# Hybrid diffusion trunk on one core: block rows exchanged and PSUM banks joined in the FFN's Strassen pairs, modulation weights and one head's scaling moved to ScalarE in the mixers

## The chip, the cores and the metric

The kernel runs on one core of a Trainium2 chip: TensorE (PE), VectorE (DVE), ScalarE (ACT), GpSimd (POOL) and SyncE (SP, which only issues transfers here), each with its own in-order instruction stream. The metric is the device time of one execution in microseconds (us). The kernel before took 2695.59, 2698.13 and 2703.82 us in three runs, median 2698.13.

## The reference

One inference step of a two-layer trunk with 640 tokens (512 latent, 128 context) of 1024 features. Each layer is a SwiGLU half-step FFN, a token mixer and another half-step FFN. Each of them reads a modulated input and is followed by a weighted residual and a layer norm:

```
def _modulation(cond, w, b):
    return (jax.nn.silu(cond) @ w + b).reshape(cond.shape[0], N_MOD, D_MODEL)

def _ffn_half(x, mod, slot, w1, w3, w2, g, b):
    h = _modulate(x, mod[:, 3 * slot], mod[:, 3 * slot + 1])
    f = (jax.nn.silu(h @ w1) * (h @ w3)) @ w2
    return _residual_post_norm(x, f, mod[:, 3 * slot + 2], FFN_RES, g, b)
```

`w1` and `w3` are 1024 x 2816. The modulation is a 1024 x 9216 product per layer for two conditioning vectors; its weights are streamed beside the other work. The mixer projects the input once, runs three groups of attention heads (A differential, B windowed with a sink logit, C latent) and one output projection. Softmax rows of group B are normalised before they multiply the values.

## The kernel before

**Layout.** Activations lie transposed, features on partitions, so that all 640 tokens are the moving side of every product. An fp32 operand is split into a high and a low part, and each product is three matmuls (`hh,wh`, `hl,wh`, `hh,wl`). The high part of a weight (`wh`) is a cast on ACT and its low part (`wl`, line 306) a subtraction on DVE, in the mixers on POOL.

**An FFN** works through its 22 tiles of 128 hidden features in six chunks, tiles 0-3, 4-6, 7-9, 10-13, 14-17 and 18-21. The first three tiles are plain products. The other 19 are done by class `Pair` (line 830): `w1` and `w3` of a tile are the two rows of a 2 x 2 block matrix, the two halves of the input features are its columns, and the activations are cut into two halves of the features and two of the tokens (`LO`, `HI`, 320 tokens each, `HN`). Seven block products p1 to p7 take the place of eight (Winograd's form), each 12 matmuls of 128x320. TensorE runs them in the order p1, p2, p4, p6, p7, p5, p3. Additions on DVE (line 858) make the four output blocks from the seven products: two of them belong to `w1` and go through SiLU on ACT, and two belong to `w3` and multiply these. The product is split into `gh` (ACT) and `gl` (DVE). After the pairs of a chunk, eight rows of `w2` products (line 485) read `gh` and `gl`; the first two rows are begun before those of the last pair are needed.

**What sets the order of these additions** is a list of deferred steps: `prod` runs `slot()` behind its 12 matmuls, and `slot()` runs each deferred step once, one product late; a step may return the next. `mods(i)` stands three times in a pair and runs the slices of a background task: in the first three of the four FFNs (`nvec`) modulations on DVE, where each `scr` (line 460) multiplies a weight tile by the conditioning and sums it, 0.716 of them a call.

**PSUM.** `bank()` takes one of four single banks in turn, `dbl()` one of two double banks. Before, a pair takes one double bank for p4 and p5, and single banks for p1, p2, p6, p7 and p3.

**A mixer** interleaves attention units with a background of projections. Modulation products (`mod_mm`, line 391) stand between them: each loads the weights of a later unit first (`mod_load`, two transfers of 256 KB, line 374) from the queue in `mod_queue`, which is SP's. SP's stream is in order and also carries weight loads (line 243) and moves between partitions (line 1256), each of which waits for its producer. In a unit of group B, `cb` (line 1715) adds the sink to the row sums, takes the reciprocal and scales the two heads' probabilities `eb` on POOL (line 1719), after which TensorE transposes them (`tr`, line 1133). Step `ptc` (line 1654) copies transposed probabilities of group C out of PSUM on ACT.

Of the kernel before, what the change touches and what calls it, by code (L numbers as in the profile page):

```python
# [105 lines left out]
def trunk_kernel(tc, I, O):  # L106
# [3 lines left out]
    with ExitStack() as es:  # L110
# [30 lines left out]
        def uid():  # L141
            cnt[0] += 1
            return cnt[0]
# [686 lines left out]
        class Pair:  # L830


            def __init__(self, h, tb, last):
# [5 lines left out]
                self.m, self.sl = u(pe_, f"pm{uid()}"), None  # L839
# [5 lines left out]
            def mms(self, out, w, b, k):  # L845
                for i, (a, c) in enumerate(((0, 0), (0, 1), (1, 0))):
                    PE.matmul(out[:, :HN], w[a][:, k, :], b[k][c], start=k == 0 and i == 0, stop=k == 3 and i == 2)  # L847

            def prod(self, out, b, post=None, w=None):
                w = w or ws.get()  # L850
                for k in range(4):
                    self.mms(out, w, b, k)
                slot()
                if post:
                    later.append(post)
# [4 lines left out]
            def c11(self, p2):  # L860
                self.sl = u(pe_, f"sl{uid()}")
                self.op(self.sl[:, LO], self.m[:, LO], p2, ALU.add)
                return lambda: S.activation(self.sl[:, LO], self.sl[:, LO], AF.Silu) and None

            def gate1(self):
                self.op(self.g[:, LO], self.g[:, LO], self.sl, ALU.mult)
                return self.half if self.last else None

            def half(self):
                split(self.gh[:, LO], self.gl[:, LO], self.g[:, LO])  # L870

            def c12(self, p3):
                self.op(self.sl[:, HI], self.m[:, LO], p3, ALU.add)
                return self.silu2

            def silu2(self):
                S.activation(self.sl[:, HI], self.sl[:, HI], AF.Silu)
                return self.gate2

            def gate2(self):  # L880
                V.tensor_tensor(out=self.g[:, HI], in0=self.g[:, HI], in1=self.sl[:, HI], op=ALU.mult)
                return self.hi

            def hi(self):
                c = HI if self.last else slice(0, T)
                S.copy(self.gh[:, c], self.g[:, c])  # L886
                return self.lo

            def lo(self):
                c = HI if self.last else slice(0, T)  # L890
                V.tensor_tensor(out=self.gl[:, c], in0=self.g[:, c], in1=self.gh[:, c].bitcast(F32), op=ALU.subtract)  # L891

            def start(self):
                p1, p2 = bank("p1"), bank("p2")
                self.prod(p1, self.b11, lambda: S.copy(self.m[:, LO], p1[:, :HN]) and None)
                self.prod(p2, self.b21, lambda: self.c11(p2))

            def run(self, mods, begun=False):
                m, op = self.m, self.op
                if not begun:  # L900
                    self.start()
                mods(0)
                p45 = dbl("p4")
                p4, p5 = p45[:, 0, :], p45[:, 1, :]
                self.prod(p4, self.t4)
                p6 = bank("p6")
                self.prod(p6, self.t2, lambda: op(m[:, LO], m[:, LO], p6, ALU.add))
                mods(1)
                p7 = bank("p7")

                def u3():
                    op(m[:, HI], m[:, LO], p7, ALU.add)
                    self.g = u(pe_, f"gf{uid()}")
                    op(self.g[:, LO], m[:, HI], p4, ALU.subtract)
                    return self.gate1
                self.prod(p7, self.t3, u3)

                def u4():
                    op(self.g[:, HI], m[:, HI], p5, ALU.add)
                    op(m[:, LO], m[:, LO], p5, ALU.add)  # L920
                self.prod(p5, self.t1, u4)
                mods(2)
                p3 = bank("p3")
                self.prod(p3, self.b22, lambda: self.c12(p3))

            def run_first(self, mods, other, ts):

                m, op = self.m, self.op
                self.start()
                mods(0)  # L930
                other.start()
                p3 = bank("p3")
                self.prod(p3, self.b22, None, ws.get(4))
                w22 = ws.get(0)
                p45, p6, p7 = dbl("p4"), bank("p6"), bank("p7")
                p4, p5 = p45[:, 0, :], p45[:, 1, :]
                wq = [ws.get(0), ws.get(0), ws.get(2), w22]
                for k in range(4):
                    for o, w, b in zip((p5, p7, p6, p4), wq, (self.t1, self.t3, self.t2, self.t4)):
                        self.mms(o, w, b, k)  # L940
                    mods(k)
                    next(ts, 0)
                slot()

                def post():
                    self.g = u(pe_, f"gf{uid()}")
# [1253 lines left out]
```

## Time and profile before

| | |
|---|---|
| three runs | 2695.59, 2698.13, 2703.82 us |
| the profiled execution | 2705.26 us |
| its span, first to last instruction | 2703.3 us |
| TensorE busy | 2555.0 us, 95% |
| VectorE busy | 2072.3 us, 77% |
| GpSimd busy | 1244.0 us, 46% |
| ScalarE busy | 1175.9 us, 43% |
| mean granted TensorE clock | 0.976 |

A granted clock of 1.00 is 2.4 GHz and 0.50 is 1.2 GHz; a mean between is a mixture of stretches at the two. "Idle before" is the time an engine waited before an instruction, with the instruction or transfer whose end released it. The profiled execution takes 7.1 us more than the median of the three runs.

### The profile page before, as it was taken

The page shows a single profiled execution, that of the slowest core. Times are in us where ns is not written, and L with a number is a line of the kernel's source. Part 1 is how long each engine was busy: PE and PEld are TensorE (multiplying, and loading weights), DVE is VectorE, ACT ScalarE, POOL GpSimd, SP SyncE. Part 2 cuts the span into 40 slices and gives each one's busy share as a digit, 9 for nine tenths or more (in the row PEclk, how much of TensorE's full clock was granted, in tenths as well). Part 3 has the DMA queues.
Part 4 walks back from the last instruction along what each step waited for, and adds up shares of the span by engine and source line. Part 5 has one row for each costly group of instructions (what it writes and reads, how often), then busy time and mean ns, then how long its engine had stood idle before and what let it go on. Part 6 is the DMA issues. An engine that isn't in the chain of part 4 may idle for free. (4 is left out here: it accounts for less than half of the span.)

```text
span 2703.3 us, 49877 instructions
## 1 busy us (share of the span) xinstructions
PE 2555.0 (95%) x18662; PEld 2453.0 (91%) x18662; DVE 2072.3 (77%) x3759; ACT 1175.9 (43%) x2596; POOL 1244.0 (46%) x973
## 2 busy tenths in 40 slices
PE   7999999899999999999989999998998999999997
PEld 6999999888778999999989999998887798999997
DVE  6599889856764879988987998898476558777776
ACT  5233333545575533333353333334545745334333
POOL 2345445522444554544555454454233456435545
PEclk9999999999999999999989999998999999999998
DMA  7333332354344223333222333323543331222222
GB/s 273 116 98 101 111 97 83 117 152 136 91 130 156 71 96 100 103 101 109 68 83 84 112 103 101 110 87 108 158 134 98 103 114 40 82 82 87 79 86 71
DMA packets 130545, 285.89 MB, mean 106 GB/s; under 512 B 16832, under 2 KB 34560, under 8 KB 129664
## 3 DMA queue, kind: packets, MB, share of 16 engines
q1 hardware_dynamic: 130304, 282.70, 33.2%
q8 instruction: 148, 2.42, 0.4%
q14 instruction: 93, 0.76, 0.1%
HBM read 254.95 MB, written 8.81 MB: 98 GB/s over the span
## 5 line engine op out<-in xcount | busy, mean ns | idle before, releaser
L306 DVE TENSOR_TENSOR wl<-wr,wh 128x512 fp32r<-128x512 f32 (+1 forms) x524 | 518.3, 1003 | 74.1 <-ACT wh L299 72.5
L299 ACT CAST wh<-wr 128x512 fp32r<-128x512 f32 (+1 forms) x570 | 333.3, 607 | 479.4 <-DMA wr<-in_w 296.9
L485 PE MATMUL o<-gh,wh 128*128 128x256 f32 (+1 forms) x1408 | 439.5, 312 | 19.4 <-ACT gh L886 11.7
L485 PE MATMUL o<-gl,wh 128*128 128x256 f32 (+1 forms) x1408 | 439.0, 312 | 1.8 <-DVE gl L478 0.3
L485 PE MATMUL o<-gh,wl 128*128 128x256 f32 (+1 forms) x1408 | 436.7, 310 | 0.0
L847 PE MATMUL p<-hh,wh 128*128 128x320 f32 x1216 | 378.4, 311 | 16.8 <-DVE pm L858 16.8
L847 PE MATMUL p<-hl,wh 128*128 128x320 f32 x1216 | 378.2, 311 | 6.2 <-DVE hl L1010 6.2
L847 PE MATMUL p<-hh,wl 128*128 128x320 f32 x1216 | 378.1, 311 | 0.0
L259 POOL TENSOR_TENSOR ws<-wr 128x512 f32<-128x512 f32 x76 | 111.5, 1468 | 545.8 <-DMA wr<-in_w 482.8
L299 ACT CAST wh<-ws 128x512 fp32r<-128x512 f32 x304 | 185.9, 621 | 361.6 <-PE p L847 153.4
L306 POOL TENSOR_TENSOR wl<-ws,wh 128x512 fp32r<-128x512 f32 x152 | 241.3, 1591 | 193.6 <-ACT wh L299 193.1
L610 DVE SCALAR_TENSOR_TENSOR x<-o,gat,x 128x128 f32<-128x128 f32 (+2 forms) x404 | 192.9, 524 | 139.6 <-PE o L485 136.6
L485 PEld LDWEIGHTS o<-gh,wh 128*128 128x128 f32 x1408 | 267.8, 190 | 23.0 <-ACT gh L886 14.5
L485 PEld LDWEIGHTS o<-gl,wh 128*128 128x128 f32 x1408 | 268.1, 190 | 6.7 <-DVE gl L891 4.8
L485 PEld LDWEIGHTS o<-gh,wl 128*128 128x128 f32 x1408 | 267.9, 190 | 0.0
L847 PEld LDWEIGHTS p<-hh,wh 128*128 128x128 f32 x1216 | 229.9, 189 | 19.0 <-issue 18.9
L847 PEld LDWEIGHTS p<-hl,wh 128*128 128x128 f32 x1216 | 230.0, 189 | 7.4 <-DVE hl L1010 7.4
L847 PEld LDWEIGHTS p<-hh,wl 128*128 128x128 f32 x1216 | 230.0, 189 | 0.3 <-DVE wl L306 0.3
L460 DVE SCALAR_TENSOR_TENSOR scr<-wv,cb 128x512 f32<-128x512 f32 x192 | 181.2, 944 | 0.0
L259 POOL TENSOR_TENSOR ws<-wr,wr 128x512 f32<-128x512 f32 x76 | 130.2, 1713 | 0.0
L259 POOL TENSOR_TENSOR ws<-wr,ws 128x512 f32<-128x512 f32 x76 | 129.9, 1709 | 0.0
L259 POOL TENSOR_TENSOR ws<-ws,wr 128x512 f32<-128x512 f32 x76 | 119.1, 1567 | 6.0
(434 smaller groups left out, 6633.9 us busy)
## 6 DMA issues: line engine op xcount, KB each, us to landing
wr<-in_w SPq DMA_DIRECT2D x176, 512.0 KB, 4.2
wm<-in_wmod SPq DMA_DIRECT2D x192, 256.0 KB, 3.9
wr<-in_w SPq DMA_DIRECT2D x128, 256.0 KB, 2.7
wv<-in_wmt SPq DMA_DIRECT2D x96, 256.0 KB, 4.0
wr<-in_w SPq DMA_DIRECT2D x64, 192.0 KB, 2.4
wr<-in_wint SPq DMA_DIRECT2D x24, 512.0 KB, 4.2
wr<-in_wo SPq DMA_DIRECT2D x16, 512.0 KB, 3.8
xd<-x SPq DMA_DIRECT2D x16, 320.0 KB, 5.1
```

The source lines that it names most:

```text
L259: G.tensor_tensor(out=o, in0=x0, in1=x1, op=op)
L299: S.copy(hl[0], src[:, c0:c1])
L306: eng.tensor_tensor(out=t2, in0=src, in1=t.bitcast(F32), op=ALU.subtract)
L460: V.scalar_tensor_tensor(out=scr, in0=w[2 * i + hf], scalar=1.0, in1=cb[:, 2 * st + hf, :], op0=ALU.mult, op1=ALU.mult, accum_out=a[:, 2 * ...
L485: PE.matmul(out[:, :cn], whl[a][:, k, :], b[:, c0:c0 + cn], start=k == 0 and i == 0, stop=k == n - 1 and i == 2)
L610: V.scalar_tensor_tensor(out=c, in0=src, scalar=gat[:, d, s:s + 1], in1=c, op0=ALU.mult, op1=ALU.add)
L847: PE.matmul(out[:, :HN], w[a][:, k, :], b[k][c], start=k == 0 and i == 0, stop=k == 3 and i == 2)
```

## The change

Five edits. (1) A pair is loaded with its two block rows exchanged (`tw[::-1]`), so that the first finished output block (from p1 and p2) and the last (from p3) belong to `w3`, and the two between to `w1`, which alone go through SiLU. The step behind p3 is now an addition and the multiplication in one. (2) p6 and p7 share a double bank as p4 and p5 do, and a pair takes both double banks, p6's first. (3) In the last pair of a chunk the second and third call of `mods` hold the `scr` steps; their credit is kept and is spent in the rows that follow. (4) In the mixers the modulation weights are loaded from ACT's queue, and two units' loads are issued ahead of the background. (5) `cb` scales the first head on ACT and the second on POOL. Functions that nothing calls any more go.

```
-                self.m, self.sl = u(pe_, f"pm{uid()}"), None
+                self.m = u(pe_, f"pm{uid()}")
...
-                self.prod(p1, self.b11, lambda: S.copy(self.m[:, LO], p1[:, :HN]) and None)
-                self.prod(p2, self.b21, lambda: self.c11(p2))
...
+                def c11():
+                    self.g = u(pe_, f"gf{uid()}")
+                    op(self.g[:, LO], m[:, LO], p2, ALU.add)
+                self.prod(p1, self.b11, lambda: S.copy(m[:, LO], p1[:, :HN]) and None)
+                self.prod(p2, self.b21, c11)
                 mods(0)
-                p45 = dbl("p4")
-                p4, p5 = p45[:, 0, :], p45[:, 1, :]
+                p67, p45 = dbl("p6"), dbl("p4")
+                p4, p5, p6, p7 = (p[:, i, :] for p in (p45, p67) for i in range(2))
                 self.prod(p4, self.t4)
-                p6 = bank("p6")
                 self.prod(p6, self.t2, lambda: op(m[:, LO], m[:, LO], p6, ALU.add))
-                mods(1)
-                p7 = bank("p7")
-
-                def u3():
+                mods(1, self.last)
+
+                def c21():
+                    self.sl = u(pe_, f"sl{uid()}")
                     op(m[:, HI], m[:, LO], p7, ALU.add)
-                    self.g = u(pe_, f"gf{uid()}")
-                    op(self.g[:, LO], m[:, HI], p4, ALU.subtract)
-                    return self.gate1
-                self.prod(p7, self.t3, u3)
-
-                def u4():
-                    op(self.g[:, HI], m[:, HI], p5, ALU.add)
+                    op(self.sl[:, LO], m[:, HI], p4, ALU.subtract)
+
+                    def silu():
+                        S.activation(self.sl[:, LO], self.sl[:, LO], AF.Silu)
+                        return gate1
+                    return silu
...
+                def c22():
+                    op(self.sl[:, HI], m[:, HI], p5, ALU.add)
                     op(m[:, LO], m[:, LO], p5, ALU.add)
-                self.prod(p5, self.t1, u4)
-                mods(2)
+                    return lambda: S.activation(self.sl[:, HI], self.sl[:, HI], AF.Silu) and None
+                self.prod(p5, self.t1, c22)
+                mods(2, self.last)
                 p3 = bank("p3")
-                self.prod(p3, self.b22, lambda: self.c12(p3))
...
+                def c12():
+                    op(self.g[:, HI], m[:, LO], p3, ALU.add)
+                    self.gate(HI)
+                    return lambda: self.split(HI if self.last else slice(0, T))
+                self.prod(p3, self.b22, c12)
...
-            def mods(when=None):
+            def mods(when=None, hold=False):
                 if vec[0]:
                     credit[0] += (4 * nvec + 4) / 95 * (1 if when is None else 1)
-                    while credit[0] >= 1:
+                    while credit[0] >= 1 and not hold:
...
-                    for hh in range(2):
-                        G.tensor_scalar(self.e[hh][:, :self.n], self.e[hh][:, :self.n], self.rs[:, hh:hh + 1], 0.0, ALU.mult, ALU.add)
+                    e0, e1 = (e[:, :self.n] for e in self.e)
+                    S.activation(e0, e0, AF.Copy, scale=self.rs[:, 0:1])
+                    G.tensor_scalar(e1, e1, self.rs[:, 1:2], 0.0, ALU.mult, ALU.add)
...
             mix_left[0] = len(modq)
+            mod_queue[0] = nc.scalar
+            mod_load(2)
...
+            mod_queue[0] = nc.sync
             mod_finish()
...
-                        r = ws.pair(*tw)
+                        r = ws.pair(*tw[::-1])
```

The order of the instructions at three places follows. A name is the tile's name, its number in the program and an index; of a double bank the name is that of the product it was taken for, so `p43560` holds p4 and p5 of one pair.

TensorE in the third FFN, the last matmuls of p2 and the first of p4 in the third pair of chunk 4, before:

```order
L847 MATMUL p23588_18706<-hh3069_15842,wh3565_18609 128x320
L847 MATMUL p23588_18706<-hl3070_15843,wh3565_18609 128x320
L847 MATMUL p23588_18706<-hh3069_15842,wl3566_18610 128x320
L847 MATMUL p43594_18745<-tvb3119_16274,wh3570_18633 128x320 [waits Activation_49]
L847 MATMUL p43594_18745<-tr3120_16275,wh3570_18633 128x320
L847 MATMUL p43594_18745<-tvb3119_16274,wl3571_18634 128x320 [waits DVE_49]
```

And after:

```order
L849 MATMUL p23541_18658<-hh3031_15804,wh3519_18565 128x320
L849 MATMUL p23541_18658<-hl3032_15805,wh3519_18565 128x320
L849 MATMUL p23541_18658<-hh3031_15804,wl3520_18566 128x320
L849 MATMUL p43548_18701<-tvb3081_16236,wh3523_18586 128x320 [waits DVE_49,Activation_49]
L849 MATMUL p43548_18701<-tr3082_16237,wh3523_18586 128x320
L849 MATMUL p43548_18701<-tvb3081_16236,wl3524_18587 128x320
```

The first matmul of p4 now waits for DVE beside ACT: its bank is the one that held p4 and p5 of the pair before, and the last to read that is a DVE addition.

VectorE in the pair before that one, from p6's addition to the last that reads p3, before (`p63564`, `p73569`, `p43560` and `p33581` are this pair's banks):

```order
L858 TENSOR_TENSOR pm3551_18547<-pm3551_18547,p63564_18607 128x320
L306 TENSOR_TENSOR wl3571_18634<-wr3544_18506,wh3570_18633 128x512
L858 TENSOR_TENSOR pm3551_18547<-pm3551_18547,p73569_18631 128x320
L858 TENSOR_TENSOR gf3580_18679<-pm3551_18547,p43560_18587 128x320
L460 SCALAR_TENSOR_TENSOR scr3244_16970,va3567_18627<-wv3497_18275,cb3121_16287 128x512
L858 TENSOR_TENSOR gf3580_18679<-gf3580_18679,sl3563_18605 128x320
L858 TENSOR_TENSOR gf3580_18679<-pm3551_18547,p43560_18587 128x320
L858 TENSOR_TENSOR pm3551_18547<-pm3551_18547,p43560_18587 128x320
L306 TENSOR_TENSOR wl3583_18685<-ws3574_18653,wh3582_18684 128x512
L858 TENSOR_TENSOR sl3563_18605<-pm3551_18547,p33581_18682 128x320
```

And after (`p63514` holds p6 and p7, `p43515` p4 and p5):

```order
L855 TENSOR_TENSOR pm3505_18500<-pm3505_18500,p63514_18543 128x320
L306 TENSOR_TENSOR wl3524_18587<-wr3498_18459,wh3523_18586 128x512
L855 TENSOR_TENSOR pm3505_18500<-pm3505_18500,p63514_18543 128x320
L855 TENSOR_TENSOR sl3533_18630<-pm3505_18500,p43515_18544 128x320
L460 SCALAR_TENSOR_TENSOR scr3205_16931,va3521_18581<-wv3452_18230,cb3083_16249 128x512
L855 TENSOR_TENSOR sl3533_18630<-pm3505_18500,p43515_18544 128x320
L855 TENSOR_TENSOR pm3505_18500<-pm3505_18500,p43515_18544 128x320
L306 TENSOR_TENSOR wl3536_18637<-ws3527_18605,wh3535_18636 128x512
L858 TENSOR_TENSOR gf3518_18562<-gf3518_18562,sl3533_18630 128x320
L855 TENSOR_TENSOR gf3518_18562<-pm3505_18500,p33534_18634 128x320
L858 TENSOR_TENSOR gf3518_18562<-gf3518_18562,sl3533_18630 128x320
```

The first multiplication by the SiLU'd half has moved from ahead of the two p5 additions to behind them; the second now stands directly behind p3's addition.

SyncE in the second mixer, among the attention units of group C, before:

```order
L1890 DMA C1qh4799_24798<-qph4585_23886 32x512
L1891 DMA C1kh4801_24800<-kph4543_23686 32x640
L1890 DMA C1ql4800_24799<-qpl4586_23887 32x512
L1891 DMA C1kl4802_24801<-kpl4544_23687 32x640
L374 DMA wm4805_24819<-in_wmod 128x512
L374 DMA wm4806_24821<-in_wmod 128x512
L374 DMA wm4812_24859<-in_wmod 128x512
```

ScalarE at the same place after, where the two `wm` transfers and the copies around them are:

```order
L1853 CAST C1qh4742_24741<-qn4556_23938 64x512 [waits Activation_49]
L1854 CAST C1kh4744_24743<-kn4630_24248 64x640 [waits Pool_49]
L1611 COPY ptc4746_24755<-tr4739_24728 128x512 [waits PE_49,Pool_49]
L374 DMA wm4748_24762<-in_wmod 128x512 [waits DMAHW1_49]
L374 DMA wm4749_24764<-in_wmod 128x512 [waits DMAHW2_49]
L1611 COPY ptc4746_24755<-t54747_24759 128x128 [waits PE_49]
L1599 ACTIVATE ec4751_24788,hs4095_21837<-sc4740_24733,uc4741_24734 128x640 [waits DVE_49]
```

The loads have left SP's stream and stand on ACT between a `ptc` copy of transposed probabilities and the next copy, which reads the bank that the modulation product writes beside it.

## Rows read from the trace of the kernel before

**Rows 1.** The page: busy time, share of the span and instructions of each engine.

```profile
PE 2555.0 (95%) x18662; PEld 2453.0 (91%) x18662; DVE 2072.3 (77%) x3759; ACT 1175.9 (43%) x2596; POOL 1244.0 (46%) x973
```

**Rows 2.** Windows over chunks 2 to 6 of each FFN: busy us, (x) instructions, granted clock.

```profile
134.13:485.40 351.27, 340.53 (x2281) 337.23 (x2281) 314.98 (x530) 128.55 (x240) 173.01 (x106) 0.99 0.31 99
999.23:1352.03 352.80, 341.55 (x2281) 337.63 (x2281) 316.01 (x530) 128.89 (x240) 172.54 (x106) 0.99 0.30 96
1474.58:1822.87 348.29, 339.14 (x2282) 336.05 (x2281) 315.51 (x530) 128.95 (x240) 171.05 (x106) 1.00 0.32 100
2331.42:2665.55 334.13, 334.13 (x2281) 334.13 (x2281) 248.57 (x388) 130.99 (x240) 161.24 (x106) 1.00 0.25 79
```

**Rows 3.** TensorE's waits over the span: us in total, times, longest.

```profile
PE p L847 <- DVE pm L858: 16.8, 8, 3.5
...
PE t L397 <- DMA wm<-in_wmod: 12.6, 13, 2.6
PE o L485 <- ACT gh L886: 11.7, 13, 1.1
PE tr L1133 <- POOL eb L1719: 9.7, 8, 2.7
...
PE tr L397 <- DMA wm<-in_wmod: 2.5, 3, 2.0
```

**Rows 4.** Timeline and window, third FFN, chunk 4, TensorE: start, us, instruction, idle before.

```profile
1621.99 0.31 PE L847 MATMUL p<-tvb,wh 128*128 128x320 f32 x1
...
1634.67 0.38 PE L847 MATMUL p<-hh,wh 128*128 128x320 f32 x1 [1.96 <-DVE pm L858]
...
1636.23 0.47 PE L847 MATMUL p<-hh,wh 128*128 128x320 f32 x1
...
1635.80:1639.20 3.40, 3.40 (x15) 3.40 (x15) 3.29 (x10) 0.00 (x0) 0.00 (x0) 0.51 0.40 124
```

**Rows 5.** Timeline, VectorE, the same place, and one gate of the first FFN.

```profile
1622.80 0.48 DVE L858 TENSOR_TENSOR gf<-gf,sl 128x320 f32<-128x320 f32 x1
...
1623.61 0.47 DVE L858 TENSOR_TENSOR pm<-pm,p 128x320 f32<-128x320 f32 x1
...
282.07 1.57 DVE L858 TENSOR_TENSOR gf<-gf,sl 128x320 f32<-128x320 f32 x1
```

**Rows 6.** Windows: a chunk of three pairs in the first FFN and in the last.

```profile
193.95:254.07 60.12, 58.85 (x398) 58.14 (x397) 55.08 (x99) 21.72 (x43) 29.67 (x19) 1.00 0.33 106
2389.45:2447.46 58.01, 58.01 (x397) 58.01 (x397) 42.50 (x71) 22.37 (x42) 26.94 (x19) 1.00 0.27 83
```

**Rows 7.** Timeline, the end of that chunk's last pair, VectorE, ScalarE and TensorE.

```profile
235.75 0.49 DVE L881 TENSOR_TENSOR gf<-gf,sl 128x320 f32<-128x320 f32 x1 [0.54 <-ACT sl L877]
...
236.28 0.46 ACT L886 CAST gh<-gf 128x320 fp32r<-128x320 f32 x1 [0.56 <-DVE gf L881]
...
236.79 0.44 PE L485 MATMUL o<-gh,wh 128*128 128x384 f32 x1 [1.06 <-ACT gh L886]
```

**Rows 8.** Timeline and window, second mixer, group A: a wait for modulation weights.

```profile
1997.78 1.14 ACT L299 CAST wh<-wr 128x512 fp32r<-128x512 f32 x2
...
2007.64 0.43 PE L397 MATMUL t<-wm,silc 128*32 128x128 f32 x4 [2.46 <-DMA wm<-in_wmod]
...
2007.80:2014.60 6.80, 5.02 (x28) 4.33 (x25) 2.00 (x5) 1.37 (x5) 4.80 (x3) 0.51 0.29 85
```

**Rows 9.** Second mixer, group C: ScalarE, TensorE, landing of modulation weights (median behind minimum).

```profile
2137.46 0.59 ACT L1654 COPY ptc<-tr 128x512 f32<-128x512 f32 x1
...
2138.76 0.65 PE L397 MATMUL t<-wm,silc 128*32 128x128 f32 x16
...
DMA to landing us min/median/max: 2.4/3.8/5.8
```

**Rows 10.** Timeline, group B: the scaling of two heads on POOL, and TensorE.

```profile
716.41 1.36 POOL L1719 TENSOR_SCALAR eb<-eb,hs 128x512 f32<-128x512 f32 x2 [2.42 <-DVE hs L1717]
...
717.15 0.67 PE L1133 MATMUL tr<-idn,eb 128*128 128x128 f32 x4 [2.73 <-POOL eb L1719]
```

More of the change, by code (lines that the diff above doesn't have):

```diff
@@ L843, in out, with prod @@
                 return self.gh, self.gl
[L845 to L850, printed above, removed]
+            def prod(self, out, b, post=None):
+                w = ws.get()
                 for k in range(4):
-                    self.mms(out, w, b, k)
+                    for i, (a, c) in enumerate(((0, 0), (0, 1), (1, 0))):
+                        PE.matmul(out[:, :HN], w[a][:, k, :], b[k][c], start=k == 0 and i == 0, stop=k == 3 and i == 2)
                 slot()
@@ L858, in op @@
                 V.tensor_tensor(out=o, in0=a, in1=b[:, :HN], op=f)
[L860 to L885, printed above, removed]
-                S.copy(self.gh[:, c], self.g[:, c])
-                return self.lo
@@ L889, in lo, with gate @@
[L889 to L893, printed above, removed]
-                p1, p2 = bank("p1"), bank("p2")
-                self.prod(p1, self.b11, lambda: S.copy(self.m[:, LO], p1[:, :HN]) and None)
-                self.prod(p2, self.b21, lambda: self.c11(p2))
[L898 to L901, printed above, removed]
+            def gate(self, c):
+                V.tensor_tensor(out=self.g[:, c], in0=self.g[:, c], in1=self.sl[:, c], op=ALU.mult)
@@ new lines, in split, with lo, run @@
+            def split(self, c):
+                S.copy(self.gh[:, c], self.g[:, c])
+                def lo():
+                    V.tensor_tensor(out=self.gl[:, c], in0=self.g[:, c], in1=self.gh[:, c].bitcast(F32), op=ALU.subtract)
+                return lo
+            def run(self, mods):
+                m, op = self.m, self.op
+                p1, p2 = bank("p1"), bank("p2")
+                def c11():
[3 more added lines that the diff above has]
+                self.prod(p2, self.b21, c11)
@@ L920, in u4, with gate1 @@
+                def gate1():
+                    self.gate(LO)
+                    return (lambda: self.split(LO)) if self.last else None
+                self.prod(p7, self.t3, c21)
+                def c22():
+                    op(self.sl[:, HI], m[:, HI], p5, ALU.add)
                     op(m[:, LO], m[:, LO], p5, ALU.add)
-                self.prod(p5, self.t1, u4)
-                mods(2)
+                    return lambda: S.activation(self.sl[:, HI], self.sl[:, HI], AF.Silu) and None
@@ L923, in run @@
+                self.prod(p5, self.t1, c22)
+                mods(2, self.last)
                 p3 = bank("p3")
-                self.prod(p3, self.b22, lambda: self.c12(p3))
[L926 to L946, printed above, removed]
-                    op(m[:, LO], m[:, LO], p6, ALU.add)
-                    op(m[:, HI], m[:, LO], p7, ALU.add)
-                    op(self.g[:, LO], m[:, HI], p4, ALU.subtract)
-                    op(self.g[:, HI], m[:, HI], p5, ALU.add)
-                    op(m[:, LO], m[:, LO], p5, ALU.add)
-                    later.append(self.gate1)
-                    return self.c12(p3)
-                later.append(post)
```

## The prediction

> **What bounds the kernel.** I read the page first. TensorE is busy 95% of the span and VectorE 77% [rows 1], so time can only come from what TensorE still waits for, or from its clock; the edits add no matmul and take none away. Then the windows. From the second chunk to the first rows behind the sixth, each FFN runs the same 2281 matmuls, in 351.27, 352.80 and 348.29 us in the first three FFNs and in 334.13 in the last, which is never idle [rows 2]. The first three thus lose 17.1 + 18.7 + 14.2 = 50.0 us. What differs is VectorE: about 315 us busy against 249, for the modulations that the last FFN doesn't run. The list of waits names TensorE's: 16.8 us in 8 waits for a pair's additions, 11.7 in 13 for `gh` at chunk ends, 15.1 in 16 for modulation weights and 9.7 in 8 for the scaled probabilities of group B [rows 3]. These four are what the change touches.
>
> **Edits 1 to 3: a new wait at p4.** The order shows that p4 of a pair now takes the bank that p4 and p5 of the pair before lay in, and waits for the VectorE addition that reads p5 last. Is that addition done in time? In the trace of before, p4 of the third pair starts at 1621.99; the addition of the second pair that it would now wait for starts at 1623.61 and takes 0.47 [rows 4, 5], so it ends at 1624.08, 2.09 late. Before, p4 had the other double bank and didn't wait. One gate of 0.48, which stood ahead of the addition, moves behind it [rows 5], and after such a wait TensorE starts some 0.15 behind the operation's end (here 1624.08 - 0.48 + 0.15 = 1623.75): a wait of 1.76. The first pair of a chunk gives no wait, its additions end 0.7 to 2.4 before the next p4. Read so pair by pair, 23 handovers are late in the first three FFNs, by 1.45 to 3.33, the worst where a gate takes 1.57 instead of 0.48 [rows 5]; in the last FFN none is.
>
> A chunk of three pairs has one late handover: six chunks, 1.3 to 2.0 each, 10.5 us. A chunk of four has two. The second must be taken with the wait that stood before it: p2 of the fourth pair waited 1.96 in this chunk (2.27 from issue to issue) for p6's addition [rows 4], and the bank it needs is now free; p4 behind it would still have been 1.58 late. The two waits together are therefore 2.27 + 1.58 - 0.33 = 3.5. Over the nine chunks this is 3.0 to 4.5 each, 34.7 us. Together 45.2.
>
> What goes. At the end of a chunk TensorE waits for SiLU, gate and high copy of the last half: the gate starts at 235.75, 0.54 after VectorE's last work, the copy at 236.28, the first row at 236.79 after 1.06 idle [rows 7]. With the addition and the gate in one step the hop to ACT and back, 0.5 to 0.6, goes, and the held `scr` steps (1.43 a chunk) free about as much on VectorE; 1.06 is less than the two, so I take these waits as gone. The held steps run in the rows, where the accumulators alone need VectorE. This cover fails if they make the row's additions late: then 15 chunks by up to 1 us come back. The chunk shown lost 60.12 - 58.01 = 2.1 [rows 6], the six of three pairs 1.4 to 3.8, 12.9 in all; they will lose 10.5. The chunks of four lose 37.1 now and will lose 34.7.
>
> The clock comes on top. The wait of 1.96 was followed, from 1636.23, by matmuls that take 0.47 instead of 0.31, for 3.4 us at a granted clock of 0.51 [rows 4], which is the lower level (1.2 GHz): about 1.7 us lost. The 50.0 contain some 8 of this, the 45.2 nothing. Waits of 1.3 to 2.0 lie between the 1.06 at chunk ends, behind which the clock stayed at 1.00 [rows 6], and this 1.96. I add 7. The FFNs then come to 52, a cost of **2 us**. Bounds: if VectorE, given rest by each wait, is never late twice in a chunk, 15 x 1.7 = 25 (24 less than now); if all 24 waits lower the clock, 45 + 24 x 1.7 = 86 (36 more). I stay near the middle, since the lateness is read from rows and only the clock isn't.
>
> The Trainium skill ("TensorE: Matmul & The Clock Gate", A second HAM failure mode: psum-queue depth-cycling) says that cycling through PSUM banks makes TensorE pause briefly between groups so often that its clock swings. By that, the joined banks would cost the upper bound. This trace agrees for one wait and disagrees for the shorter ones at chunk ends, whose rows show the clock up.
>
> **Edit 4: modulation weights on ScalarE's queue.** In group A of the second mixer TensorE waits 2.46 and then 1.78 for one unit's weights, and the next 6.8 us are at 0.51 [rows 8]. The load stood on SP's queue behind moves that wait for their producers. On ACT it will stand behind the cast that starts at 1997.78 [rows 8] and ends at 1998.92; with a landing of 3.8, 5.8 at most [rows 9], it is there by 2004.7, and the use was at 2007.64 less 2.46 = 2005.2. So I read each unit of groups A and B: ACT comes to its load 4 to 24 us before use. About 13.6 of the 15.1 go [rows 3], and about 7 of lost clock with them. In group C it is otherwise. There ACT reaches the load behind a `ptc` copy that starts at 2137.46 and takes 0.59, and the product starts at 2138.76 [rows 9]: 0.7 for a transfer that takes 2.4 at the least, 3.8 mostly. TensorE waits some 1.7 to 3 there, and ten units of both mixers have 0.7 to 3.1. Their deficits sum to about 10 us, as far as one wait doesn't help the next; with 1.5 for the clock: -20.6 + 11.5 = **-9 us**. Bounds: no gain in A and B leaves +11; no new wait leaves -21. A load costs ACT its issue, 0.4 to 1 us by SP's rows for the same transfer, in an engine that is busy 43% [rows 1]; what it delays is the `pt` copies, which are read 4 us or more after they end. I price it at +1.
>
> The Trainium skill ("DMA: Bandwidth & Descriptors", Issuing engines are not separate DMA queues) says that transfers started from several engines run on the same 16 DMA engines, and that this saves only the time to start them. By this rule edit 4 would bring nothing. The trace shows a wait ahead of the start, which the rule leaves out, so I give it the smaller chance.
>
> **Edit 5.** TensorE waits 2.73 for two scalings that take 1.36 together on POOL [rows 10]. Side by side, one of them goes from the chain, 0.6 to 0.7 us. Eight waits of 9.7 [rows 3] lose about 4.8, less 1 where ACT is in other work when the reciprocal is ready; the longest two were followed by a low clock, and may not be now. **-4 us**, between -9 and +3 (ACT's stream waits for VectorE's reciprocal 32 times and holds its copies back).
>
> **Sum.** +2 - 9 + 1 - 4 = -10 us on the profiled 2705.3. Against the median of the runs, 2698.1, this gives **2688**. A measurement tells about 0.3% from no change, 8.1 us: below 2690.0 is faster and above 2706.2 slower.
>
> **Rivals.**
> (a) *The single turn of the joined bank* decides. Each of some 24 waits falls in the same place, and if the clock drops behind more than half of them the cost is 45 + 13 x 1.7 = 67, 17 more than now; as TensorE's shorter waits move the chunk's end, VectorE's held steps then make the rows late too, some 5. With -12 in the mixers that is +10, 2708; all 24 drops give 36 + 5 - 12 = +29, 2727. For it speaks the 1.96 with its drop [rows 4], against it the 1.06 without [rows 6, 7]. It is slower, by more than a measurement can miss, from some 12 drops on (45 + 20 - 50 + 5 - 12 = 8).
> (b) *Weights come no earlier*: edit 4 gains as much in A and B as it loses in C. Then +2 + 1 - 4 leaves 2697, no change. For it speaks the 0.7 of [rows 9], against it the 8.7 of [rows 8].
> (c) *VectorE catches up in its rests*: one wait a chunk, 25 in place of 50, and the mixers as forecast: 2698 - 25 - 12 = 2661. For it speaks that VectorE has 36 us to spare in each window [rows 2]; against it, that it is late in the third handover by its own backlog, whatever TensorE waited at the second.
> (d) *The exchange doesn't shorten the chunk's end*, since VectorE is late there itself: +12 on the forecast, 2700. This lies within (b)'s result, and I count it there.
>
> **Chances and range.** The forecast 0.42, (a) 0.20, (b) with (d) 0.20, (c) 0.18. The forecast's own range is 2678 to 2698, so of its 0.42 some 0.27 are faster and 0.15 no change. (a) gives 0.18 slower and 0.02 no change, (b) 0.15 no change and 0.05 faster, (c) 0.18 faster. Faster 0.50, no change 0.30, slower 0.20. The range leaves out the far half of (a) and of (c): 2662 to 2712.
>
> **What the new profile would show.** Waits of p4 for the second p5 addition, 1.3 to 2 us, once in chunks of three pairs and twice in chunks of four, in the first three FFNs only; no wait of p2 for p6's addition; hardly any wait for `gh` on ACT. The window of 2281 matmuls between 345 and 355. In the mixers, no wait for weights before group C, and up to ten of 1 to 3 us in it. Shorter waits for `eb`. The forecast is wrong if the p4 waits are few (then it is faster than said) or are followed by the lower clock (slower), or if waits for weights stay in groups A and B.

## The result and the profile after

The changed kernel takes 2718.07 us, the median of 8 runs (2710.53 to 2724.58); the kernel before took 2697.06 (8 runs). The ratio is 1.0079, interval 1.0064 to 1.0094: **21 us slower**, where 10 us faster was forecast. 2718 lies outside the range given too.

The profiled execution of the changed kernel took 2711.05 us (span 2709.2, clock 0.977), one of its shortest runs; that of before, 2705.26, was longer than all 8 of its timed runs. The pair differs by 5.8 where the medians differ by 21, so no stretch is judged from these two profiles alone: below, sums are compared over the profiles of several kernels.

The page of the changed kernel, its row of engines:

```profile
PE 2547.3 (94%) x18662; PEld 2443.7 (90%) x18662; DVE 2040.3 (75%) x3759; ACT 1193.0 (44%) x2628; POOL 1226.3 (45%) x941
```

32 scalings have gone from POOL to ACT, beside [rows 1]. TensorE's waits in the changed kernel (total, times, longest):

```profile
PE o L485 <- DVE pm L855: 29.6, 15, 3.3
...
PE sa L1557 <- issue: 11.6, 2, 6.3
...
PE tr L1090 <- ACT eb L1676: 6.5, 6, 2.6
...
PE tr L1090 <- ACT ms L425: 3.2, 3, 1.6
...
PE t L397 <- DMA wm<-in_wmod: 2.3, 3, 1.3
PE p L849 <- DVE pm L855: 2.3, 5, 0.5
```

Against [rows 3]: the 12.6 us for weights are 2.3, the waits of a pair for additions fell from 16.8 to 2.3, and the 11.7 for `gh` are nearly gone. In their place stand 29.6 us in which the first `w2` row waits for an addition (`pm`), once in each of chunks 2 to 6 of the first three FFNs, and 11.6 of a score product (`sa`) whose operands come late (the profile says "issue"; the section on edit 4 shows what it is).

The windows of the 2281 matmuls, and the chunk of three pairs that [rows 6] show:

```profile
134.08:486.65 352.57, 340.10 (x2282) 336.66 (x2281) 308.60 (x530) 128.09 (x240) 171.11 (x106) 0.99 0.31 99
1002.56:1355.99 353.43, 340.04 (x2281) 335.60 (x2281) 309.81 (x530) 128.07 (x240) 171.91 (x106) 1.00 0.30 95
1476.60:1827.53 350.93, 338.21 (x2282) 334.11 (x2282) 309.88 (x529) 127.59 (x239) 172.34 (x106) 1.00 0.31 99
```

```profile
194.13:255.36 61.23, 59.04 (x398) 58.00 (x397) 55.19 (x98) 21.54 (x42) 29.01 (x19) 1.00 0.32 104
```

The three windows come to 1056.9 against 1052.4 in [rows 2], with the clock where it was; TensorE's idle time in them (the window less PE's busy time) is 38.6 in place of 31.1. The chunk takes 61.23 against 60.12.

### The profile page after: what moved, and what is told of

The parts are those of the page before. It is cut to its first block, busy times and chain, and to the rows that moved or that the text cites. A ratio compares the mean times of both kernels' runs of the same rounds, so it can differ in the third digit from the quotient of the medians.

```text
span 2709.2 us, 49747 instructions
## 1 busy us (share of the span) xinstructions
PE 2547.3 (94%) x18662; PEld 2443.7 (90%) x18662; DVE 2040.3 (75%) x3759; ACT 1193.0 (44%) x2628; POOL 1226.3 (45%) x941
## 5 line engine op out<-in xcount | busy, mean ns | idle before, releaser
L485 PE MATMUL o<-gh,wh 128*128 128x256 f32 (+1 forms) x1408 | 442.9, 315 | 36.3 <-DVE pm L855 29.6
L460 DVE SCALAR_TENSOR_TENSOR scr<-wv,cb 128x512 f32<-128x512 f32 x192 | 170.7, 889 | 0.5
L855 DVE TENSOR_TENSOR pm<-pm,p 128x320 f32<-128x320 f32 x228 | 109.1, 478 | 40.3 <-PE p L849 40.3
L858 DVE TENSOR_TENSOR gf<-gf,sl 128x320 f32<-128x320 f32 x152 | 103.7, 682 | 36.1 <-ACT sl L890 28.1
```

The lines of the kernel that those rows point to most:

```text
L460: V.scalar_tensor_tensor(out=scr, in0=w[2 * i + hf], scalar=1.0, in1=cb[:, 2 * st + hf, :], op0=ALU.mult, op1=ALU.mult, accum_out=a[:, 2 * ...
L485: PE.matmul(out[:, :cn], whl[a][:, k, :], b[:, c0:c0 + cn], start=k == 0 and i == 0, stop=k == n - 1 and i == 2)
L855: V.tensor_tensor(out=o, in0=a, in1=b[:, :HN], op=f)
L858: V.tensor_tensor(out=self.g[:, c], in0=self.g[:, c], in1=self.sl[:, c], op=ALU.mult)
```

## The experiments

The edits are numbered as in the section on the change. A ratio is to the kernel before on the same chip. "FFN" is the sum of the three windows of 2281 matmuls, "mixers" the time from the last product of a pair in one FFN to the first in the FFN behind the mixer, both mixers together, each from the kernel's one profile.

| kernel | edits | median us | ratio (95%) | FFN | mixers |
|---|---|---|---|---|---|
| before | | 2697.1 | 1 | 1052.4 | 959.8 |
| changed | 1 to 5 | 2718.1 | 1.0079 (1.0064 to 1.0094) | 1056.9 | 965.2 |
| ffn_only | 1 to 3 | 2710.9 | 1.0051 (1.0032 to 1.0070) | 1064.6 | 960.4 |
| mix_only | 4, 5 | 2705.1 | 1.0036 (1.0020 to 1.0053) | 1046.9 | 962.8 |
| swap_only | 1 | 2699.8 | 1.0013 (0.9994 to 1.0032) | 1045.7 | 956.0 |
| join_only | 2 | 2697.5 | 1.0000 (0.9983 to 1.0017) | 1049.4 | 954.7 |
| swap_join | 1, 2 | 2697.9 | 1.0004 (0.9990 to 1.0018) | 1054.7 | 962.2 |
| hold_only | 3 | 2706.2 | 1.0040 (1.0022 to 1.0058) | 1056.0 | 954.4 |
| load_only | 4 | 2695.0 | 0.9988 (0.9974 to 1.0002) | 1048.9 | 954.7 |
| eb_only | 5 | 2710.5 | 1.0050 (1.0030 to 1.0069) | 1051.4 | 965.3 |
| no_eb | 1 to 4 | 2708.8 | 1.0044 (1.0027 to 1.0061) | 1061.0 | 961.3 |
| row_banks | 1 to 5, rows' banks | 2715.7 | 1.0063 (1.0045 to 1.0081) | 1060.4 | 966.2 |
| ahead_on_sp | 1 to 5, ahead on SP | 2708.2 | 1.0039 (1.0027 to 1.0051) | 1061.7 | 960.6 |
| load_ahead_sp | 4, ahead on SP | 2682.1 | 0.9946 (0.9929 to 0.9964) | 1047.7 | 938.9 |
| best | 1, 2, 4, ahead on SP | 2688.7 | 0.9964 (0.9950 to 0.9979) | 1052.9 | 950.9 |
| sp_swap | 1, 4, ahead on SP | 2686.7 | 0.9969 (0.9952 to 0.9986) | 1048.4 | 948.5 |
| sp_hold | 3, 4, ahead on SP | 2690.6 | 0.9985 (0.9973 to 0.9996) | 1057.2 | 944.2 |

The changes of the single parts add up: 0.04% (1 and 2 together) + 0.40 (3) - 0.12 (4) + 0.50 (5) = 0.82%, and 0.79 was measured.

**The halves.** mix_only is the kernel before with these lines, ffn_only the changed kernel without them:

```
-                    for hh in range(2):
-                        G.tensor_scalar(self.e[hh][:, :self.n], self.e[hh][:, :self.n], self.rs[:, hh:hh + 1], 0.0, ALU.mult, ALU.add)
+                    e0, e1 = (e[:, :self.n] for e in self.e)
+                    S.activation(e0, e0, AF.Copy, scale=self.rs[:, 0:1])
+                    G.tensor_scalar(e1, e1, self.rs[:, 1:2], 0.0, ALU.mult, ALU.add)
...
+            mod_queue[0] = nc.scalar
+            mod_load(2)
...
+            mod_queue[0] = nc.sync
```

> Edits 1 to 3 alone, mixers as before. Theory A (the loss lies in the mixers): ratio 0.997 to 1.003, and TensorE has the 15 waits of a first w2 row for the pair's addition (about 30 us) in place of the waits at p2 and for gh (28 us). Theory B (the joined banks cost the time): ratio 1.005 to 1.009, most of the +21 us.

> Edits 4 and 5 alone, FFNs as before. Theory A (SP's moves wait for transfers that ACT issues late): ratio 1.004 to 1.009, with the two waits of 5 to 6 us ahead of sa and some 20 us in which SP's rp moves wait for wm transfers. Theory B: the waits for wm are gone and nothing takes their place, ratio 0.994 to 1.000.

Neither half gains: 0.51% and 0.36% slower. What was forecast for the second half, -12 us, came out at +8. The 0.51% lies in the range that was expected if the joined banks cost the time; join_only, below, shows that they don't.

**The first `w2` row of a chunk.** The changed kernel, with the first row on two single banks and the second on the double one:

```
-                    p = dbl("o") if d == 0 else [bank("o"), bank("o")]
+                    p = [bank("o"), bank("o")] if d == 0 else dbl("o")
```

> The changed kernel with the first w2 row of a chunk on two single banks and the second on a double bank. If the first row's wait for the addition that reads p7 is the FFN's cost: the 29.6 us in 15 waits fall under 8, and the time is 15 to 22 us under the changed kernel's. If other work on VectorE is late there as well (gh, gl), the wait turns up under these names and the gain is under 8 us.

The wait went, and little time with it. TensorE's waits in row_banks:

```profile
PE o L485 <- ACT gh L862: 18.2, 15, 1.5
...
PE o L485 <- DVE gl L865: 7.8, 15, 0.5
```

The 29.6 were no separate loss: with the bank free, the row waits 26.0 for a `gh` and `gl` that come later than before's `gh` (11.7 us).

**The parts of edits 1 to 3, each alone.** join_only:

```
-                p45 = dbl("p4")
-                p4, p5 = p45[:, 0, :], p45[:, 1, :]
+                p67, p45 = dbl("p6"), dbl("p4")
+                p4, p5, p6, p7 = (p[:, i, :] for p in (p45, p67) for i in range(2))
...
-                p6 = bank("p6")
...
-                p7 = bank("p7")
```

> Edit 2 alone: p6 and p7 joined, block rows and mods as before. Theory J (the joined banks carry the FFN's +14 us): 25 to 30 us of waits of a first w2 row for the addition that reads p7, p2's 16.8 us gone, ratio 1.002 to 1.006. Theory S (the exchange carries it): ratio 0.998 to 1.001.

No difference that can be measured. swap_only has the new order of steps in a pair without these banks, the core of it:

```
-                        r = ws.pair(*tw)
+                        r = ws.pair(*tw[::-1])
```

> Edit 1 alone: block rows exchanged, banks and mods as before. Theory J: TensorE's waits for gh fall from 11.7 us to under 6, ratio 0.996 to 1.000. Theory S (with the exchange both SiLUs and the first gate come behind p7 and p5 and stand ahead of p3's addition, so that gh is no earlier): gh 10 us or more, ratio 1.001 to 1.006.

None here either. hold_only:

```
-                mods(1)
+                mods(1, self.last)
...
-                mods(2)
+                mods(2, self.last)
...
-            def mods(when=None):
+            def mods(when=None, hold=False):
...
-                    while credit[0] >= 1:
+                    while credit[0] >= 1 and not hold:
```

> Edit 3 alone: the last pair of a chunk holds the scr steps. If these stand in front of the chunk's last additions: waits for gh fall by 3 to 6 us, ratio 0.997 to 0.999. If they are made good in the rows, where they make additions of w2 rows late instead: ratio 1.000 to 1.003.

Holding the steps costs 0.40% by itself, above both ranges that were expected. TensorE's waits in hold_only, in the chunk of [rows 6] (which now takes 61.50):

```profile
PE o L485 <- ACT gh L886: 1.1, 1, 1.1
PE p L847 <- DVE sl L858: 0.7, 1, 0.7
```

Its timeline, TensorE at the chunk's end and VectorE from there on:

```profile
237.25 0.44 PE L485 MATMUL o<-gh,wh 128*128 128x384 f32 x1 [1.06 <-ACT gh L886]
...
239.50 0.68 DVE L460 SCALAR_TENSOR_TENSOR scr<-wv,cb 128x512 f32<-128x512 f32 x1
240.10 0.08 DVE L460 DVE_READ_ACCUMULATOR scr<-wv,cb 128x1 f32 x1
240.22 0.69 DVE L460 SCALAR_TENSOR_TENSOR scr<-wv,cb 128x512 f32<-128x512 f32 x1
...
261.11 0.48 DVE L858 TENSOR_TENSOR sl<-pm,p 128x320 f32<-128x320 f32 x1
```

And the kernel before, the first such addition of the next chunk:

```profile
259.31 0.47 DVE L858 TENSOR_TENSOR sl<-pm,p 128x320 f32<-128x320 f32 x1
```

The wait for `gh` is the same 1.06 as in [rows 7]: these steps had not been what made it late, since VectorE waits there for ScalarE (0.54 idle in [rows 7]). In the rows, where two of them now stand one behind the other, they delay VectorE, which begins the next chunk's additions 1.80 later by these rows, of which 0.85 is that chunk's own later start (the windows of the chunk before it end at 254.07 and at 254.92). Over the span hold_only has 4.8 us in 7 waits of a product for `sl` where before has 0.8 in one, and 1.7 in 8 waits of a row for `x` where before has 0.4 in two.

swap_join is ffn_only without the held steps; sp_swap and sp_hold are the kernel load_ahead_sp (below) with the lines of swap_only and of hold_only. The edit of swap_join against ffn_only:

```
-                    while credit[0] >= 1 and not hold:
+                    while credit[0] >= 1:
```

> Edits 1 and 2 together, steps not held, mixers as before. By the FFN part (+13.8) less the held steps (+10.8): +3 us, ratio 1.000 to 1.002. If the exchange and the joined banks make a cost together that neither has alone (0 and +3.5): 1.003 or more.

> The version with weights on ACT and the loads ahead on SP (ratio 0.9946), and the exchange of block rows on top, banks single as before. If the exchange by itself is worth what its FFN stretches show (4 us less in three FFNs): ratio 0.992 to 0.994. If it costs what its time alone said (+3.5 us): 0.995 to 0.997.

> The same version with the held steps on top, rows and banks as before. If held steps cost by themselves, whatever stands beside them: 7 to 11 us over it, ratio 0.997 to 0.999, the first three FFNs 7 us longer than in kernels without them. If the +11 measured for them alone was spread between runs: within 4 us, 0.993 to 0.996.

The seven profiles with held steps have FFNs of 1056.0 to 1064.6 (mean 1059.7), the ten without 1045.7 to 1054.7 (mean 1049.8). The groups don't overlap; the means differ by 9.9 us, but not by edit 3 alone: five of the seven also have edits 1 and 2, and only two of the ten. Like with like, hold_only and sp_hold (1056.0 and 1057.2) stand some 7 above the five profiles with none of edits 1 to 3 (mean 1049.5), and the five with edits 1 to 3 (mean 1060.9) as much above swap_join and best (1054.7 and 1052.9). TensorE's idle time in the windows is 32.8 and 33.1 in hold_only and sp_hold, 26.0 to 31.1 in those five. By the medians the held steps cost 11 us in hold_only and 8.6 in sp_hold against load_ahead_sp (10.5 by the ratios): some 5 of it is found as waits, and where the rest goes is not shown.

**Edit 5 alone, and all but edit 5.** eb_only has of the lines shown for mix_only these, and no_eb is the changed kernel without them:

```
-                    for hh in range(2):
...
+                    S.activation(e0, e0, AF.Copy, scale=self.rs[:, 0:1])
+                    G.tensor_scalar(e1, e1, self.rs[:, 1:2], 0.0, ALU.mult, ALU.add)
```

> Edit 5 alone: one head scaled on ACT, weight loads on SP. As forecast: waits of tr for eb fall from 9.7 us to 5 to 7, ratio 0.997 to 0.9995. If ACT comes late to the scaling, or its copies come late behind it: the same 8 to 10 us, ratio 1.000 to 1.002, and then most of the mixers' +8 us is edit 4's less than thought.

> The changed kernel without edit 5 (both heads on POOL again). If ACT's waits for the reciprocal and the copies behind them are edit 5's cost: 8 to 14 us under the changed kernel, ratio 1.003 to 1.005, and in group B no waits of TensorE for ms or kn copies. If the mixers lose by the lanes alone: within 4 us of the changed kernel, 1.006 to 1.008.

0.50% slower alone, above both ranges that were expected, and 0.35% better without it (1.0079 to 1.0044). eb_only, timeline of group B in the first mixer:

```profile
709.99 0.72 ACT L1719 ACTIVATE eb<-eb,hs 128x512 f32<-128x512 f32 x1 [2.61 <-DVE hs L1717]
710.62 0.84 ACT L1142 COPY pt<-tr 128x512 f32<-128x512 f32 x2
...
712.79 0.28 ACT L425 COPY ms<-tr 128x128 f32<-128x128 f32 x1
...
713.13 0.66 PE L1133 MATMUL tr<-idn,eb 128*128 128x128 f32 x4 [1.56 <-ACT ms L425]
...
718.59 1.12 PE L1133 MATMUL tr<-idn,eb 128*128 128x128 f32 x4 [1.33 <-ACT eb L1719]
```

ScalarE stands idle for 2.61 until VectorE has the reciprocal (`hs`), and its copies stand behind: the `ms` copy for which TensorE then waits 1.56 comes 2.8 after the scaling began. ScalarE's row for this wait in eb_only, the whole span:

```profile
ACT eb L1719 <- DVE hs L1717: 31.4, 25, 3.2
```

Two stretches of group B, one in each mixer, the same matmuls in both kernels. Windows of before, then of eb_only:

```profile
710.02:790.04 80.02, 69.21 (x670) 53.52 (x669) 57.07 (x145) 52.51 (x162) 40.74 (x57) 0.98 0.30 90
2050.08:2127.68 77.60, 69.58 (x637) 52.78 (x637) 53.72 (x139) 49.10 (x152) 38.64 (x54) 0.94 0.28 83
```

```profile
710.08:795.12 85.04, 73.50 (x670) 55.45 (x669) 55.66 (x145) 62.54 (x179) 30.19 (x43) 0.94 0.28 85
2047.99:2131.12 83.13, 69.78 (x637) 53.29 (x637) 54.33 (x140) 58.95 (x172) 28.05 (x39) 0.92 0.26 77
```

5.0 and 5.5 us are lost here. In the first stretch TensorE's busy time grows from 69.21 to 73.50 at a granted clock of 0.94 in place of 0.98: between these two profiles the difference is matmuls at the lower clock. That edit 5 lowers it is not shown: swap_only, load_only, sp_swap and best, with both scalings on POOL, have the 0.94 there too and take 82.0 to 82.8 us, and TensorE's idle time is 10.3 to 11.7 in all 17 profiles. In the second stretch the busy time is the same and the idle time grew, from 8.0 to 13.4; it is 6.4 to 9.9 in the twelve profiles with both scalings on POOL and 12.1 to 14.4 in the five with one on ScalarE. The two stretches together come to 154.6 to 160.2 in the twelve and to 163.9 to 168.2 in the five (means 157.5 and 165.8).

**Edit 4 alone, and with the two units ahead on SP.** load_only is the kernel before with edit 4; load_ahead_sp differs from it by this, and ahead_on_sp from the changed kernel by the same:

```
-            mod_queue[0] = nc.scalar
             mod_load(2)
+            mod_queue[0] = nc.scalar
```

> Edit 4 alone: modulation weights on ACT's queue, everything else as before. By edits 4 and 5 together (+8 us) less edit 5 alone (+13.6): -5 us, ratio 0.997 to 0.999; TensorE's waits for weights in the mixers under 4 us instead of 15, and 5 to 12 us ahead of sa in their place. If edit 5 and edit 4 cost one another nothing and the lanes alone explain the mixers: ratio 1.001 to 1.003.

> Edit 4 with the two units' loads ahead of the mixer issued by SP. If SP's moves behind ACT's late transfers are what takes back the gain: no wait of 5 us or more ahead of sa, 6 to 12 us under edit 4 alone, ratio 0.993 to 0.997. If not: as edit 4 alone, within 3 us.

> The changed kernel with the two units' loads ahead of each mixer issued by SP and only the later ones by ACT. Theory A: both waits of 5 to 6 us ahead of sa go, 10 to 14 us less than the changed kernel. If those waits have another cause, they stay, within 3 us.

load_only gains nothing that can be measured; with the ahead loads on SP it is 0.54% faster than before, **2682.1 us, which beats both kernels**, and the changed kernel is better by 10 us (ahead_on_sp). TensorE's waits in load_only name the place:

```profile
PE sa L1600 <- issue: 6.7, 1, 6.7
...
PE sa L1600 <- DMA rp<-l: 5.0, 1, 5.0
```

In load_ahead_sp all waits for `rp` come to 2.8 us, so that some 9 of the 13 us between the two are these waits.

The same place in the changed kernel, timeline of SP's and ScalarE's queues and TensorE:

```profile
565.99 3.14 SPq L1220 DMA_DIRECT2D rp<-h  x2
569.17 4.22 SPq L1220 DMA_DIRECT2D rp<-l  x2
...
570.20 0.38 ACTq L374 DMA_DIRECT2D wm<-in_wmod  x1
...
570.62 1.43 ACTq L374 DMA_DIRECT2D wm<-in_wmod  x3
...
576.91 0.87 PE L1557 MATMUL sa<-rp,rp 128*128 128x320 f32 x2 [5.32 <-issue]
```

And in load_ahead_sp:

```profile
565.82 1.22 SPq L1263 DMA_DIRECT2D rp<-h  x2
...
574.46 2.01 SPq L374 DMA_DIRECT2D wm<-in_wmod  x4
...
570.01 0.53 PE L1600 MATMUL sa<-rp,rp 128*128 128x320 f32 x2 [1.50 <-DMA rp<-l]
```

Two pairs of SP's small moves (`rp`) take 3.14 and 4.22 to issue in place of 1.22. SP's own waits here, in the changed kernel:

```profile
SPq L1220 <- DMA wm<-in_wmod: 3.1, 1, 3.1
SPq L1220 <- DMA rp<-h: 2.1, 1, 2.1
```

In the program the transfers of both queues take turns on the same eight semaphores (two of them, `DMAHW1` and `DMAHW2`, stand in the order rows), and a transfer waits for the one that had its semaphore before. The second pair waits for a `wm` load that ScalarE issues only at 570.20, behind its copies, and that lands at 572.87. The first waits for one of SP's own earlier moves: in the program's order the four loads have every second semaphore, so SP comes round to the same one after some four moves of its own in place of eight. Over the span SP's list of waits gives 22.0 us in 9 waits for `wm` loads. It gives load_ahead_sp 17.6 in 7, but at places where TensorE doesn't wait: the total alone would not have shown the difference.

**Putting the gains together.** best is the changed kernel without edits 3 and 5, with the ahead loads on SP, thus ahead_on_sp with both scalings on POOL (the lines of no_eb) and

```
-                    while credit[0] >= 1 and not hold:
+                    while credit[0] >= 1:
```

> Edits 1, 2 and 4 with the loads ahead on SP, without the held steps and with both heads on POOL. If held steps (+11) and head scaling (+14) are the two that cost, and the rest is neutral or better: ratio 0.994 to 0.999. If the exchange with the joined banks carries the FFN's cost: 1.002 or more.

It gains 0.36%, less than load_ahead_sp's 0.54 without edits 1 and 2. The intervals touch; nothing here says that edits 1 or 2 help.

## Why the prediction was wrong

By halves: edits 1 to 3 were put at +2 and measured +14; edits 4 and 5 at -12 and measured +8. The two misses, 12 and 20 us, account for the 30 between forecast and result. By parts: edits 1 and 2 measured +1 (swap_join), edit 3 +11, edit 4 -3 (its interval contains no change) and edit 5 +14. Three steps thus carry the miss: the cover for the held steps (4), the loads ahead that the forecast of edit 4 left out (6), and the price of ScalarE's wait (7). Two more steps of the FFN's sum failed and cancelled out (2 and 3). The chances, added up as said, give 0.32 for no change and 0.18 for slower, not 0.30 and 0.20.

1. **What bounds the kernel** was read rightly: the matmuls stayed, and what is seen to move is TensorE's waits; its clock differs by stretches between profiles, in group B also among kernels without edit 5.

2. **The new wait at p4, 45 us, did not come: a failed step.** Its premise was that p4 takes the bank of p4 and p5 of the pair before. So says the sentence behind the first order fence, and it is wrong. In the program's allocation the double banks alternate: over four pairs p6 and p7 lie in bank 2, 0, 2, 0 and p4 and p5 in 0, 2, 0, 2. The wait on `DVE_49` that the order shows is for an earlier addition, the one that reads p7; it is p6, 12 matmuls later, that needs the readers of p5. The changed kernel's timeline, VectorE and TensorE:

```profile
460.08 0.47 DVE L855 TENSOR_TENSOR pm<-pm,p 128x320 f32<-128x320 f32 x1
...
460.70 0.39 PE L849 MATMUL p<-tvb,wh 128*128 128x320 f32 x1 [0.46 <-DVE pm L855]
...
462.21 0.48 DVE L855 TENSOR_TENSOR pm<-pm,p 128x320 f32<-128x320 f32 x1
...
462.83 0.53 PE L849 MATMUL p<-tva,wh 128*128 128x320 f32 x2
```

p4 starts 0.15 behind the end of p7's addition (460.55), after 0.46; p6 0.14 behind that of p5's second (462.69), some 0.3 late. All such waits come to 2.3 us.

3. **The chunk's end: failed, and the largest cost in the FFNs that was not foreseen.** The forecast took the waits for `gh` as gone, since a hop to ScalarE goes and the held steps free VectorE. The changed kernel at the end that [rows 7] show:

```profile
231.21 0.98 ACT L299 CAST wh<-wr 128x384 fp32r<-128x384 f32 x2 [3.14 <-PE p L849]
...
231.75 0.56 DVE L306 TENSOR_TENSOR wl<-wr,wh 128x384 fp32r<-128x384 f32 x1 [2.23 <-ACT wh L299]
232.22 0.48 DVE L855 TENSOR_TENSOR pm<-pm,p 128x320 f32<-128x320 f32 x1
...
232.85 0.36 PE L485 MATMUL o<-gh,wh 128*128 128x256 f32 x1 [1.56 <-DVE pm L855]
...
234.69 0.51 ACT L299 CAST wh<-wr 128x384 fp32r<-128x384 f32 x1 [2.50 <-DMA wr<-in_w]
235.10 0.47 ACT L890 ACTIVATE sl<-sl 128x320 f32<-128x320 f32 x1
...
235.60 0.49 DVE L858 TENSOR_TENSOR gf<-gf,sl 128x320 f32<-128x320 f32 x1 [1.04 <-ACT sl L890]
236.04 0.49 DVE L855 TENSOR_TENSOR gf<-pm,p 128x320 f32<-128x320 f32 x1
...
237.15 0.46 ACT L862 CAST gh<-gf 128x320 fp32r<-128x320 f32 x1 [0.56 <-DVE gf L858]
...
237.58 0.39 PE L485 MATMUL o<-gl,wh 128*128 128x256 f32 x1 [0.55 <-DVE gl L865]
```

Two things were missed. The first row's double bank `o` is the one in which p6 and p7 lay, so the row waits for p7's addition, which itself stands behind a weight split whose cast TensorE released late (1.56; 29.6 over 15 chunks). And both SiLUs now come behind the p7 and p5 additions, here behind a cast that waited 2.50 for its weights; the gate that waits for the first stands ahead of p3's addition on VectorE. `gh` begins at 237.15 where before it began at 236.28 [rows 7]. This is rival (d); it was priced inside "no change".

The 45 us at p4 and the 7 of clock didn't come; the 29.6 at the chunks' ends, and 16.0 by which TensorE's busy time in the three windows exceeds three times the last FFN's, were not in the sum. By the windows of the changed kernel the three FFNs lose 54.5 us (1056.9 less 3 x 334.13) where the forecast said 52: that the two lie so near is luck.

4. **The held steps: failed cover.** "They run in the rows, where the accumulators alone need VectorE" named the price if wrong, up to 15 us; the runs give 10 to 11. Some 5 of it is seen, mostly at another place than was said: the rows' own additions are hardly late (1.7 us in 8 waits in hold_only), the next chunk's are (4.8 in 7). Where the other half goes stays open.

5. **The clock, +7 in the FFNs: not seen.** The windows stay at 0.99 to 1.00, behind waits up to 3.3 us. The sign came out as in rival (a), but by another way: neither the joined bank (ratio 1.0000) nor its clock did it. The rule on bank cycling of the Trainium skill ("TensorE: Matmul & The Clock Gate", A second HAM failure mode: psum-queue depth-cycling) is not borne out for these banks: the mean clock of join_only's profile is 0.982, of before's 0.976.

6. **Edit 4, -9 and +1: right in A and B and wrong in what it adds.** The waits for weights went, 15.1 to 2.3 + 0.6. The ten late units of group C were mostly not late; at the place of [rows 9] one is, by 1.31. In the changed kernel, TensorE and ScalarE's queue:

```profile
2140.86 1.74 ACTq L374 DMA_DIRECT2D wm<-in_wmod  x2
...
2143.87 0.63 PE L397 MATMUL t<-wm,silc 128*32 128x128 f32 x12 [1.31 <-DMA wm<-in_wmod]
```

Not counted were the two units ahead, which hold up SP's moves from a queue that is itself late. That took 13 us of a gain of 16, load_only against load_ahead_sp. With these two on SP edit 4 gives -16 by the medians (2698.26 to 2682.06). The Trainium skill's rule ("DMA: Bandwidth & Descriptors", Issuing engines are not separate DMA queues), by which another queue would bring nothing, doesn't hold for a load that stood behind waiting moves: the 15.1 us of waits for weights are 1.7 in load_ahead_sp. What the two units ahead ran into, semaphores that two queues share, is not what that rule speaks of.

7. **Edit 5, -4 (range -9 to +3): measured +14, the mis-sized term of the mixers.** The forecast saw that ScalarE waits for the reciprocal 32 times and took 1 us for it. It is 31.4 us of idle ScalarE, and its copies are late for TensorE; the wait for `eb` fell only from 9.7 to 7.7, since it was the reciprocal, not the second scaling, that came late.

**Open.** Why edit 1 costs what it seems to, by the ratios 3.5 us in swap_only and 6 in sp_swap against load_ahead_sp, neither clear of the intervals, while swap_only's FFNs are the shortest of all: where the rest lengthens is not shown. Of edit 5's 14 us some 8 to 10 lie in the two stretches of group B; the waits of the second, some 5, are the part that stands apart from every profile without it. The single profiles' mixers scatter by about 8 us among kernels with the same mixer code (954.4 to 962.2), so no smaller difference there is read from one.

## What to carry to other kernels

An operation that waits for another engine is priced by what stands behind it on its own engine: moving it to an idle engine can lay that wait on the engine's next copies, as it did here 25 times of 32. Before a wait is laid on a bank, read which tile it really follows, and check the program's allocation rather than the name. Where queues take turns on the same semaphores, as in this program, a load that stands early in the program on a queue that is late holds up the transfers of the other queue; issue such loads from the queue that is on time.

## What was not expected of the hardware

SP's moves waited for loads issued on ScalarE's queue, and for their own earlier ones while the loads had half of the semaphores: 1.22 us a pair became 4.22 and 3.14. And a clock of 0.94 in place of 0.98 over 85 us of group B cost 4.3 us of matmul time, where waits of up to 3.3 in the FFNs left the clock at 0.99 to 1.00. What lowers it there, in eb_only as in four kernels without edit 5, no run here tells.
